# Hybrid retention and pooling block: the swish gate in seven-product units, retention and pooling input through DRAM, the retention merge ahead of the pooling branch

## The chip, the cores and the metric

The kernel runs on one core of a Trainium2 chip. The metric is device time in microseconds (us); the median of plain runs is compared, and one further execution is profiled. Times of one execution come from that profile.

## What is computed

One decoder block for one sequence of S = 1024 tokens, D = 1024 channels, all in float32. After an RMS norm with gain, one projection gives queries, keys and values of 4 retention heads, a swish gate g, 512 pooling channels pu and two gates of 1024:

```python
h = rmsnorm(x, ln_mix);  z = h @ w_in            # q | k | v | g | pu | gate_logits
ret   = retention_chunkwise(rotary(q) * 128**-0.5, rotary(k), v)      # chunks of 128
ret_n = groupnorm_per_head(ret) * gn_gain
y_ret = (silu(g) * ret_n) @ w_ret_up
y_pool = multiscale_pool(pu, pool_w, pool_scale) @ w_pool_up          # causal windows 2, 4, 8, 16
x = x + (sigmoid(g_A) * y_ret + sigmoid(g_B) * y_pool) @ w_o
x = x + relu(rmsnorm(x, ln_mlp) @ w_up)**2 @ w_down
out = rmsnorm(x, ln_f)
```

## The kernel before

Activations are kept feature-major: 128 features on the partitions, 1024 tokens in two halves of 512 (`sl`, `half`). A float32 operand is carried as a pair, a rounded high half (`split_pair`, L134, a copy on ScalarE) and a low half (L135, a subtraction on VectorE), and a product takes three passes: high by high, high by low, low by high (`PASSES`, `product`, L121). So a 128x512 result over 1024 inputs takes 8 x 3 = 24 matmuls (`feature_major`), that is 48 for both halves of a feature tile. The norm's 1/rms is not applied to h; it is in `R1`, by which results are multiplied afterwards.

`seven` (L177) is the other way to make products, one Strassen-like unit: a 1024x256 weight block is read as 2x2 blocks `a11, a12, a22, a21`, their sums s1 to s4 are made on VectorE (L188, into a tile of their own, `sum_...`), and seven products of 4 x 3 = 12 matmuls accumulate into the banks X, Y, Z and V: 84 matmuls make two feature tiles, which would take 96. The operands on the other side are the quarters of h and four sums of them, `hx`, which `mixed_blocks(k)` makes for k = 0 to 3: it loads two feature tiles of x again (`xw`, 1 MB, on POOL's DMA queue, L514, into a buffer of the weights' pool), scales them on ScalarE (L517), and makes four sums and their halves (L525, L135). A unit's results are read from the banks in `done`. With `late=True`, for the first unit, the first four products run over k = 0 to 2 first, and over k = 3 afterwards.

The stages, with their place in the profiled execution:

- 0 to 274 us: queries and keys (`rotary`), values (`ps_v`), and the retention of four heads (`retain`). Its end takes the group norm: statistics on VectorE, a power instruction on POOL (L441), the scaling on VectorE (L444), 64 transposes on TensorE (`ps_rt`, L454), and the result stays in SBUF as `retn`, 8 features.
- 225 to 371 us: `swish(f)` for 8 features (`ps_g`, 384 matmuls), between them `pool(g)` for 4 windows (`ps_pu`, 192 matmuls, then the window sums on VectorE), `pool_mix` (`ps_pw`, 24 matmuls) and `mixed_blocks`. The gated retention goes to `ret_dram`, the pooled result to `yp_dram`.
- 366 to 533 us: 8 gate units (`gates`, `ps_Xsg`, `ps_Ysg`, `ps_Zsg`, `ps_Vsg`; 672 matmuls). Their sigmoids go to `sg_dram`.
- 535 to 578 us: pooling merge (`ps_yp`, 192 matmuls), multiplied by its gate from `sg_dram` into `m` (L625). `ypf`, the pooled result, is loaded within the last gate unit.
- 578 to 665 us: retention merge (`ps_yr`, 384 matmuls), with `ret` loaded from `ret_dram` (L630), multiplied by its gate and added (L650, L651) into `mixT`.
- 665 to 753 us: output projection (`ps_o`, 384 matmuls) and the second norm: sums over the squares by matmul (`sums_b`), 1/rms on VectorE and POOL (`rstd_b`, L146, L147), spread by transposes (`spread_b`, L153).
- 754 to 1056 us: 16 seven-product units `up`, whose squared ReLU goes to `act_dram`; 1056 to 1380 us: the down projection by the same scheme (`ps_dnX` and so on, L854) and the last norm (`spread_z`).

Instructions are written stage by stage; the tile framework orders them on each engine by its own simulated timeline and sets the waits on buffers. The buffers are pools: `wpool` 4 buffers of 1 MB (weights, `xw`, `ret`), `rpool` 2 (raw weights), `apool` with tags `h` 16, `r` 16 and `a` 9 buffers of half a megabyte, PSUM 5 banks `mm` and 3 `aux`. DMA loads are queued on SP, stores and the `xw` loads on POOL.

## Time and profile before

| what | value |
|---|---|
| median of 3 plain runs | 1387.05 us (1386.79 to 1387.15) |
| profiled execution | 1388.35 us |
| its span | 1386.2 us |
| TensorE busy | 1365.0 us, 6584 instructions |
| VectorE busy | 967.1 us, 1590 instructions |
| ScalarE busy | 542.8 us, 903 instructions |
| mean granted TensorE clock | 0.995 of full speed |

A busy time is the sum of the stretches in which an engine runs an instruction. PE stands for TensorE, PEld for its weight loads, DVE for VectorE, ACT for ScalarE, POOL for GpSimd, SP for the queue that issues loads. "<-" in a wait points to what ended it; names in the trace have their numbers left out, so `w_sg` is any weight half of a gate unit.

### The profile page before, as it was taken

The numbers are of one execution on the slowest core, as the hardware profiler recorded it, in microseconds if no ns is written. First come the engines' busy times: TensorE is split into PE (matmuls) and PEld (weight loads), VectorE is DVE, ScalarE is ACT, GpSimd is POOL, SyncE is SP. The second block draws the span as 40 slices with busy tenths as digits, with TensorE's granted clock in tenths as the row PEclk, the third lists the DMA queues.
The fourth block names the chain that finished last, engine by engine and source line by source line (L and its number), as shares of the span: only waits on it lengthen the run. The fifth ranks groups of instructions, "written<-read, shape, count | busy, mean of one in ns | idle before, by whom it ended". The sixth has DMA issues, their size and how long they took to land.

```text
span 1386.2 us, 17348 instructions
## 1 busy us (share of the span) xinstructions
PE 1365.0 (98%) x6584; PEld 1146.2 (83%) x6584; DVE 967.1 (70%) x1590; ACT 542.8 (39%) x903; POOL 77.9 (6%) x136
## 2 busy tenths in 40 slices
PE   9999999999999999999999999999999999999997
PEld 6998999888788887888887888888887788888886
DVE  5766666778766746645467888777776977589574
ACT  6232324343333333322344343343332544444371
POOL 0000000100000000000000111101110000000000
PEclk9999999999999999999999999999999999999998
DMA  9111111223323328534322344334449986779431
GB/s 357 50 60 49 33 42 47 99 91 122 137 81 118 122 99 312 181 122 137 137 76 83 112 166 164 141 140 168 167 168 355 408 312 234 251 266 319 146 122 61
DMA packets 63490, 216.66 MB, mean 156 GB/s; under 512 B 7152, under 2 KB 9200, under 8 KB 59824
## 3 DMA queue, kind: packets, MB, share of 16 engines
q1 hardware_dynamic: 47568, 158.66, 32.7%
q0 software_dynamic: 15696, 56.89, 10.8%
q8 instruction: 51, 0.84, 0.2%
q14 instruction: 31, 0.25, 0.1%
q10 hardware_dynamic: 144, 0.03, 0.0%
HBM read 163.12 MB, written 52.43 MB: 155 GB/s over the span
## 4 chain that ended last, share of the span: by engine, by line
PE 91%; issue 5%; DVE 2%; DMA 1%; ACT 1%; POOL 0%; POOLq 0%; DVEq 0%; SPq 0%; ACTq 0%
PE ps_v L121 7%; PE ps_o L121 6%; PE ps_yr L121 6%; PE ps_Xup L195 6%; PE ps_Zup L195 6%; PE ps_dnX L854 6%; PE ps_dnZ L854 6%; PE ps_Vup L195 6%; PE ps_dnV L854 6%; PE ps_qT L121 3%; PE ps_g L121 3%; PE ps_yp L121 3%; PE ps_kT L121 3%; PE ps_Yup L195 3%; PE ps_Xsg L195 3%
## 5 line engine op out<-in xcount | busy, mean ns | idle before, releaser
L121 PE MATMUL ps_v<-w_v_hi,hT 128*128 128x256 f32 x512 | 95.9, 284 | 0.0
L854 PE MATMUL ps_dnX<-db,da 128*128 128x512 f32 x384 | 93.3, 390 | 2.6 <-ACT db L134 1.6
L195 PE MATMUL ps_Xup<-mv,w_up 128*128 128x512 f32 x384 | 93.8, 390 | 1.3 <-DVE w_up L135 1.3
L195 PE MATMUL ps_Vup<-mv,w_up 128*128 128x512 f32 x384 | 92.8, 389 | 0.0
L195 PE MATMUL ps_Zup<-mv,w_up 128*128 128x512 f32 x384 | 92.7, 389 | 0.0
L121 PE MATMUL ps_g<-hT,w_g 128*128 128x512 f32 x384 | 91.1, 392 | 0.0
L121 PE MATMUL ps_o<-mixT,w_o 128*128 128x512 f32 x384 | 87.5, 389 | 0.0
L854 PEld LDWEIGHTS ps_dnX<-db,da 128*128 128x128 f32 x384 | 71.8, 188 | 18.7 <-ACT db L134 2.0
L121 PE MATMUL ps_yr<-retT,w_ret 128*128 128x512 f32 x384 | 87.2, 389 | 0.0
L195 PEld LDWEIGHTS ps_Xup<-mv,w_up 128*128 128x128 f32 x384 | 71.9, 188 | 16.6 <-DVE w_up L135 1.8
L195 PEld LDWEIGHTS ps_Zup<-mv,w_up 128*128 128x128 f32 x384 | 72.1, 188 | 15.0
L121 PEld LDWEIGHTS ps_yr<-retT,w_ret 128*128 128x128 f32 x384 | 72.1, 188 | 15.0
L195 PEld LDWEIGHTS ps_Vup<-mv,w_up 128*128 128x128 f32 x384 | 72.1, 188 | 14.9
L121 PEld LDWEIGHTS ps_o<-mixT,w_o 128*128 128x128 f32 x384 | 72.0, 188 | 15.0
L121 PEld LDWEIGHTS ps_g<-hT,w_g 128*128 128x128 f32 x384 | 71.9, 189 | 14.7
L121 PEld LDWEIGHTS ps_v<-w_v_hi,hT 128*128 128x128 f32 x512 | 80.8, 192 | 0.0
L121 PE MATMUL ps_v<-w_v_lo,hT 128*128 128x256 f32 x256 | 72.7, 284 | 0.0
L730 ACT ACTIVATE act<-act 128x512 f32<-128x512 f32 x64 | 40.4, 632 | 71.7 <-DVE act L729 71.5
L134 ACT ACTIVATE w_up<-sum_up 128x512 fp32r<-128x512 f32 x64 | 40.2, 631 | 66.3 <-PE ps_Zup L195 27.3
L121 PE MATMUL ps_qT<-hT,w_qT 128*128 128x512 f32 x192 | 48.5, 398 | 1.4 <-ACT hT L138 1.1
L134 ACT ACTIVATE w_up<-raw_up 128x512 fp32r<-128x512 f32 x48 | 30.1, 630 | 49.1 <-PE ps_Zup L195 24.9
L121 PEld LDWEIGHTS ps_v<-w_v_lo,hT 128*128 128x128 f32 x256 | 49.1, 192 | 0.0
(251 smaller groups left out, 2811.6 us busy)
## 6 DMA issues: line engine op xcount, KB each, us to landing
...
raw_up<-in_w_up_dram SPq DMA_DIRECT2D x16, 1024.0 KB, 5.0
raw_sg<-in_w_gate_dram SPq DMA_DIRECT2D x8, 1024.0 KB, 4.9
...
```

Of the source, the lines that this page charges most:

```text
L121: nc.tensor.matmul(ps, stationary(k, sa), moving(k, sb), start=i == 0, stop=i == n - 1)
L134: nc.scalar.activation(dst[:, 0, :], src, AF.Copy)
L195: nc.tensor.matmul(ps, ws[x][:, sa, k * P : (k + 1) * P], moving[x][k][:, sb, :], start=start and k == 0 and n == 0, stop=k == 3 and n == ...
L730: nc.scalar.activation(dst, dst, AF.Square)
L854: nc.tensor.matmul(banks[i][:, c0 : c0 + n], w[:, sa, i * P : (i + 1) * P], x[:, sb, c0 : c0 + n], start=start and j == 0 and m == 0, stop ...
```

## The change

1. `seven` has no tile for the sums: s3 goes into a temporary tile with p1, u2 and u4, and s1, s2, s4 overwrite the raw blocks a21, a11 and a12. T2's product makes s3, s1 and s2, in this order. The up units use the same function.
2. The swish gate's projection is made by four more units: `mixer_unit(i)`, i = 0 to 3 for the swish gate, 4 to 11 for the two gates, all from one weight array `w_mix`. In `done`, a swish unit multiplies by R1 and the sign (one operation), takes the sigmoid on ScalarE, multiplies the normalized retention by gain and sigmoid, and by z.
3. `retain` returns the normalized chunks, with the scaling on ScalarE (and a small `nb` on VectorE). `transposed` writes each `retn` feature to `retn_dram`, on POOL's queue; the swish units load them back into their output tiles on the same queue. For head 3 it stands behind the pooling input and the mixed blocks, which now fill the time of this head's retention.
4. `pool_input(g)` makes only the pooling channels u, to `u_dram`. The windows and `ps_pw` have moved into the retention merge's loop, `pool(f // 2)` behind each odd f, and give `ypT` directly.
5. The retention merge (`ps_yr`) runs ahead of the pooling merge (`ps_yp`). `load_ret` is called within unit 11; the second gate is loaded in pairs (`sgb`) in the pooling merge, which adds and makes `mixT`.

As built, TensorE has 48 matmuls fewer, VectorE 32 additions or products more, ScalarE 48 activations more, POOL's queue 15 DMAs more and SP's 3 fewer.

```diff
@@ seven
-        sums = w_tile(f"sum_{name}", F32).rearrange("p (b j) -> p b j", b=4)
-        s1, s2, s3, s4 = (sums[:, i, :] for i in range(4))
+        tmp = w_tile(f"tmp_{name}", F32).rearrange("p (b j) -> p b j", b=4)
+        p1, u2, u4, s3 = (tmp[:, i, :] for i in range(4))
+        s1, s2, s4 = a21, a11, a12
...
-            T2: (Y, (s2, (s1, a21, a22), (s2, s1, a11))),
+            T2: (Y, (s2, (s3, a11, a21), (s1, a21, a22), (s2, s1, a11))),
             T1: (Z, (s1,)),
-            T3: (V, (s3, (s3, a11, a21))),
+            T3: (V, (s3,)),
@@ retain
+            nb = stat.tile([P, 4], F32, tag="nb", name=f"nb{h}_{half}", bufs=2)
+            nc.vector.scalar_tensor_tensor(nb, mv[:, :, 0], -1.0, rs, ALU.mult, ALU.mult)
             for t in range(4):
-                nc.vector.tensor_scalar(
-                    rt[:, t, :], rt[:, t, :], mv[:, t, 0:1], rs[:, t : t + 1],
-                    ALU.subtract, ALU.mult,
+                nc.scalar.activation(
+                    rt[:, t, :], rt[:, t, :], AF.Identity,
+                    bias=nb[:, t : t + 1], scale=rs[:, t : t + 1],
                 )
             rn.append(rt)
+        return rn
+
+    def transposed(h, rn):
...
-            retn.append(dst)
+            nc.gpsimd.dma_start(retn_dram[2 * h + e], dst)
@@ pooling input and mixed blocks
+    def pool_input(g):
+        w = load_piece(a["w_fm"][8 + g], f"w_pu{g}")
+        u = a_tile("a", f"u{g}")
+        for half in range(2):
...
+            feature_major(ps, w, hT, half)
+            nc.vector.tensor_tensor(u[:, sl], ps, R1[:, sl], ALU.mult)
+        nc.gpsimd.dma_start(u_dram[g], u)
...
-    for f in range(KT):
-        swish(f)
-        if 1 <= f <= 4:
-            pool(f - 1)
-        if 2 <= f <= 5:
-            pool_mix(f - 2)
-        if 1 <= f <= 4:
-            mixed_blocks(f - 1)
...
+    pool_input(0)
+    for g in range(1, 4):
+        pool_input(g)
+        mixed_blocks(g - 1)
+    mixed_blocks(3)
+    transposed(NH - 1, rn)
@@ units
+    def mixer_unit(i, late=False, after=None):
+        swish = i < 4
+        f0 = i if swish else (i - 4) // 4 * KT + i % 4
         tiles = (f0, f0 + 4)
+        o = [a_tile("h", f"mx{i}_{f}") for f in tiles]
+        if swish:
+            for m, f in enumerate(tiles):
+                nc.gpsimd.dma_start(o[m], retn_dram[f])
...
+            if swish:
+                nc.vector.scalar_tensor_tensor(z, y, sign, R1[:, sl], ALU.mult, ALU.mult)
+                nc.scalar.activation(sig, z, AF.Sigmoid)
+                nc.vector.scalar_tensor_tensor(
+                    dst, dst, vec[:, V_GNG + f : V_GNG + f + 1], sig, ALU.mult, ALU.mult
+                )
+                nc.vector.tensor_tensor(dst, dst, z, ALU.mult)
...
+    for i in range(12):
+        mixer_unit(i, late=i == 0, after=load_ret if i == 11 else None)
@@ merges
+    for f in range(KT):
+        w = load_piece(a["w_ret"][f], f"w_ret{f}")
+        m = a_tile("a", f"m{f}")
+        nc.sync.dma_start(m, sg_dram[f])
+        for half in range(2):
...
+            feature_major(ps, w, retT, half)
+            nc.vector.tensor_tensor(m[:, sl], m[:, sl], ps, ALU.mult)
+        mixed.append(m)
+        if f % 2:
+            pool(f // 2)
...
+            sg = w_tile(f"sgb{f}", F32).rearrange("p (i t) -> p i t", i=2)
+            nc.sync.dma_start(sg, sg_dram[KT + f : KT + f + 2].rearrange("i p t -> p i t"))
```

Where the order moves, three places. First VectorE (DVE) ahead of the first unit. Before, these rows stand among the last swish halves (`ps_g`, `retn`), with the sums and halves of gate unit 0 (`sum_sg0`, `w4_sg0`) and the last mixed operand (`hx6_3`):

```order
L537 TENSOR_TENSOR ps_g6_0_3322<-ps_g6_0_3322,R1_128 128x512
L135 TENSOR_TENSOR hx6_3_3236<-xw3_3219,hx6_3_3236 128x512
L188 TENSOR_TENSOR sum_sg0_3454<-raw_sg0_3452 128x512
L539 SCALAR_TENSOR_TENSOR retn3_0_2466<-retn3_0_2466,vec_101,sig6_0_3347 128x512
L188 TENSOR_TENSOR sum_sg0_3454<-raw_sg0_3452 128x512
L188 TENSOR_TENSOR sum_sg0_3454<-sum_sg0_3454,raw_sg0_3452 128x512
L542 TENSOR_TENSOR retn3_0_2466<-retn3_0_2466,ps_g6_0_3322 128x512
L188 TENSOR_TENSOR sum_sg0_3454<-raw_sg0_3452,sum_sg0_3454 128x512
L135 TENSOR_TENSOR w4_sg0_3475<-sum_sg0_3454,w4_sg0_3475 128x512
```

After, the same place has the last u product (`ps_pu3_1`) and the mixed operands of k = 3 among the sums of unit 0 (`tmp_mx0`, `raw_mx0`):

```order
L189 TENSOR_TENSOR tmp_mx0_2842<-raw_mx0_2840 128x512
L135 TENSOR_TENSOR hx5_3_2795<-xw3_2786,hx5_3_2795 128x512
L508 TENSOR_TENSOR xw3_2786<-xw3_2786 128x512
L189 TENSOR_TENSOR raw_mx0_2840<-raw_mx0_2840 128x512
L492 TENSOR_TENSOR u3_2712<-ps_pu3_1_2739,R1_128 128x512
L135 TENSOR_TENSOR hx4_3_2799<-xw3_2786,hx4_3_2799 128x512
L135 TENSOR_TENSOR w0_mx0_2847<-raw_mx0_2840,w0_mx0_2847 128x512
L135 TENSOR_TENSOR hx6_3_2803<-xw3_2786,hx6_3_2803 128x512
L189 TENSOR_TENSOR raw_mx0_2840<-raw_mx0_2840 128x512
L135 TENSOR_TENSOR w4_mx0_2862<-raw_mx0_2840,w4_mx0_2862 128x512
```

The swish products that stood between the operands of the units are gone from there, and the xw chain of k = 3 now stands directly ahead of the first unit's low half `w0_mx0`.

Second SP's queue at the end of the units. Before, the pooled results (`ypf`) and the gates (`m`) follow the last unit's weights:

```order
L179 DMA raw_sg7_4404<-in_w_gate_dram 128x2048
L604 DMA ypf0_4464<-yp_dram_2497 128x1024
L604 DMA ypf1_4472<-yp_dram_2497 128x1024
L604 DMA ypf2_4480<-yp_dram_2497 128x1024
L604 DMA ypf3_4488<-yp_dram_2497 128x1024
L620 DMA m0_4575<-sg_dram_3449 128x1024
```

After, it is the gated retention (`ret`, 1 MB each) and the gates of the retention branch:

```order
L179 DMA raw_mx11_4368<-in_w_mix_dram 128x2048
L569 DMA ret0_4427<-ret_dram_2834 128x2048
L569 DMA ret1_4441<-ret_dram_2834 128x2048
L614 DMA m0_4566<-sg_dram_2835 128x1024
L614 DMA m1_4625<-sg_dram_2835 128x1024
L569 DMA ret2_4455<-ret_dram_2834 128x2048
L614 DMA m2_4711<-sg_dram_2835 128x1024
L614 DMA m3_4770<-sg_dram_2835 128x1024
L614 DMA m4_4859<-sg_dram_2835 128x1024
L614 DMA m5_4918<-sg_dram_2835 128x1024
L569 DMA ret3_4469<-ret_dram_2834 128x2048
L614 DMA m6_5010<-sg_dram_2835 128x1024
```

The last quarter of the retention (`ret3`) is asked for behind six gate tiles.

Third TensorE at the first up unit. Before, the sums of the second half's squares (`sums_b1`) stand among matmuls of up units 0 and 1, and their spread follows after V, X and other groups:

```order
L163 MATMUL sums_b1_6083<-ones_97,sums2_5419 128x1 x4
L195 MATMUL ps_Vup0_6109<-mv5_3_6051,w5_up0_6149 128x512
L195 MATMUL ps_Xup1_6250<-mv0_0_5554,w0_up1_6254 128x512
L195 MATMUL ps_Xup1_6250<-mv0_1_5717,w0_up1_6254 128x512 x3
L195 MATMUL ps_Xup1_6250<-mv0_2_5880,w0_up1_6254 128x512 x3
L195 MATMUL ps_Vup0_6109<-mv5_3_6051,w5_up0_6149 128x512 x2
L195 MATMUL ps_Xup1_6250<-mv0_3_6043,w0_up1_6254 128x512 x3
L195 MATMUL ps_Xup0_6106<-mv1_3_6061,w1_up0_6169 128x512
L153 MATMUL spread_b1_6091<-ident_92,rstd_b1_6088 128x128 x4
L195 MATMUL ps_Yup0_6107<-mv4_0_5569,w4_up0_6124 128x512 x3
```

After, X of up unit 0 comes first, and four matmuls of Z and V stand between the sums and their spread:

```order
L153 MATMUL spread_b0_6138<-ident_92,rstd_b0_6135 128x128 x4
L196 MATMUL ps_Xup0_6165<-mv0_0_5615,w0_up0_6169 128x512 x3
L196 MATMUL ps_Xup0_6165<-mv0_1_5778,w0_up0_6169 128x512 x3
L196 MATMUL ps_Xup0_6165<-mv0_2_5941,w0_up0_6169 128x512 x3
L196 MATMUL ps_Xup0_6165<-mv0_3_6104,w0_up0_6169 128x512 x3
L163 MATMUL sums_b1_6144<-ones_97,sums2_5480 128x1 x4
L196 MATMUL ps_Zup0_6167<-mv3_0_5619,w3_up0_6196 128x512 x2
L196 MATMUL ps_Vup0_6168<-mv5_0_5623,w5_up0_6208 128x512 x2
L153 MATMUL spread_b1_6152<-ident_92,rstd_b1_6149 128x128 x4
L196 MATMUL ps_Yup0_6166<-mv4_0_5630,w4_up0_6184 128x512 x3
```

Between the sums and their spread stood 14 wide matmuls; now there are 4.

## Rows read from the trace of the kernel before

**Rows 1.** The page, part 1: busy us, share of the span, instructions.

```profile
PE 1365.0 (98%) x6584; PEld 1146.2 (83%) x6584; DVE 967.1 (70%) x1590; ACT 542.8 (39%) x903; POOL 77.9 (6%) x136
```

**Rows 2.** The page, part 4: chain that ended last, by engine.

```profile
PE 91%; issue 5%; DVE 2%; DMA 1%; ACT 1%; POOL 0%; POOLq 0%; DVEq 0%; SPq 0%; ACTq 0%
```

**Rows 3.** Waits of PE: what waited for what, us in total, times, longest.

```profile
PE spread_z L153 <- POOL rstd_z L147: 3.0, 2, 1.9
PE ps_yp L121 <- ACT w_po L94: 1.7, 1, 1.7
PE ps_dnX L854 <- ACT db L134: 1.6, 1, 1.6
PE ps_Ysg L195 <- ACT w_sg L134: 1.4, 1, 1.4
...
PE ps_dnX L854 <- DVE db L135: 1.1, 2, 0.8
...
PE ps_Zsg L195 <- DVE w_sg L135: 0.5, 1, 0.5
PE ps_pw L356 <- DVE pooled L135: 0.4, 2, 0.2
```

**Rows 4.** Timeline of PE: start, us, instructions; a key projection, transposes, a value matmul.

```profile
66.40 11.07 PE L121 MATMUL ps_kT<-hT,w_kT 128*128 128x512 f32 x48
77.31 0.60 PE L368 MATMUL ps_kt<-ident,kT 128*128 128x128 f32 x4
77.67 0.36 PE L121 MATMUL ps_v<-w_v_hi,hT 128*128 128x256 f32 x1
```

**Rows 5.** Windows: stretch, length; busy PE, PEld, DVE, ACT, POOL; PEclk; DMA share; GB/s.

```profile
368.70:371.70 3.00, 3.00 (x9) 2.32 (x8) 2.97 (x6) 0.76 (x2) 0.00 (x0) 0.50 0.13 52
534.70:537.70 3.00, 2.97 (x13) 2.45 (x14) 1.83 (x2) 1.72 (x3) 0.64 (x2) 1.00 0.84 244
756.70:759.70 3.00, 2.92 (x13) 2.40 (x14) 3.00 (x7) 0.93 (x2) 0.00 (x0) 1.00 0.12 49
1075.30:1078.30 3.00, 2.62 (x10) 1.88 (x11) 3.00 (x6) 2.23 (x5) 1.60 (x3) 1.00 1.05 416
224.60:366.40 141.80, 139.99 (x672) 116.63 (x670) 106.00 (x183) 56.47 (x91) 10.60 (x16) 1.00 0.30 103
366.40:532.60 166.20, 165.31 (x719) 136.04 (x720) 109.89 (x171) 64.41 (x105) 9.05 (x17) 0.99 0.34 123
```

**Rows 6.** Timelines of PE and PEld: the first gate unit, then the first up unit.

```profile
367.55 3.87 PE L195 MATMUL ps_Ysg<-hx,w_sg 128*128 128x512 f32 x10 [0.41 <-DVE w_sg L135]
371.22 2.09 PE L121 MATMUL ps_g<-hT,w_g 128*128 128x512 f32 x7
...
756.78 2.58 PE L195 MATMUL ps_Xup<-mv,w_up 128*128 128x512 f32 x10 [1.35 <-DVE w_up L135]
...
769.67 0.41 PEld L153 LDWEIGHTS spread_b<-ident,rstd_b 128*128 128x128 f32 x4 [0.26 <-POOL rstd_b L147]
```

**Rows 7.** Timeline of DVE: sums and low halves of gate units.

```profile
366.81 1.89 DVE L135 TENSOR_TENSOR w_sg<-sum_sg,w_sg 128x512 fp32r<-128x512 f32 x3
...
419.72 1.29 DVE L188 TENSOR_TENSOR sum_sg<-raw_sg 128x512 f32<-128x512 f32 x2
```

**Rows 8.** DMA issues (KB each, median us to landing), and the landings of ret.

```profile
xw<-in_xT_dram POOLq DMA_DIRECT2D x4, 1024.0 KB, 5.6
...
ret<-ret_dram SPq DMA_DIRECT2D x4, 1024.0 KB, 5.0
...
DMA to landing us min/median/max: 4.8/5.0/9.9
```

**Rows 9.** Timeline of POOL: the power instruction of the second norm.

```profile
768.21 1.41 POOL L147 TENSOR_TENSOR rstd_b<-rstd_b,nhalf 128x4 f32<-128x4 f32 x1 [12.98 <-DVE rstd_b L146]
```

**Rows 10.** Groups by line: busy, mean ns of one, idle before and what ended it.

```profile
L444 DVE TENSOR_SCALAR rn<-rn,mv,rs 128x256 f32<-128x256 f32 x32 | 11.0, 409 | 0.2
...
L517 ACT ACTIVATE xw<-xw,vec 128x1024 f32<-128x1024 f32 x8 | 8.8, 1142 | 30.8 <-DMA xw<-in_xT_dram 30.8
```

More of the change, by code (lines that the diff above doesn't have):

```diff
@@ L199, in mult @@
                     )
-        tmp = rpool.tile([P, 2, HALF], F32, tag="raw", name=f"tmp_{name}")
-        p1, u2 = tmp[:, 0, :], tmp[:, 1, :]
-        u4 = rpool.tile([P, HALF], F32, tag="raw", name=f"u4_{name}")
         X, Y = mm_bank(f"ps_X{name}"), aux_bank(f"ps_Y{name}")
@@ L358, in exact @@
             )
-    retn = []
+    retn_dram = dram_tile("retn_dram", (KT, P, S))
     def retain(h, qT, kT, v):
@@ L580, in done @@
             dst, f = o[m][:, sl], tiles[m]
+            sign = -1.0 if m else 1.0
+            if swish:
+                t = rpool.tile([P, 2, HALF], F32, tag="raw", name=f"sw{f}_{half}")
+                z, sig = t[:, 0, :], t[:, 1, :]
+            else:
+                z = ps if add is None else dst
             y = ps
             if add is not None:
-                nc.vector.tensor_tensor(dst, add, ps, ALU.add)
-                y = dst
-            nc.vector.tensor_tensor(y, y, R1[:, sl], ALU.mult)
@@ L611, in block_kernel, with load_ret @@
-    for i in range(KT):
-        gates(i)
-    mixed = []
+                nc.gpsimd.dma_start(ret_dram[f // 2, :, f % 2, :] if swish else sg_dram[f], o[m])
+        seven(f"mx{i}", a["w_mix"][i], hx, done, late=late, after=after)
+    retT = []
+    def load_ret():
+        for p2 in range(KT // 2):
+            r2 = w_tile(f"ret{p2}", F32).rearrange("p (i t) -> p i t", i=2)
+            nc.sync.dma_start(r2, ret_dram[p2])
+            for i in range(2):
+                retT.append([])
+                for half in range(2):
+                    dst = pair_tile("h" if p2 < 2 else "r", f"retT{2 * p2 + i}_{half}")
+                    split_pair(dst, r2[:, i, half * HALF : (half + 1) * HALF])
+                    retT[-1].append(dst)
@@ new lines, in block_kernel, with pool @@
+    for i in range(12):
+        mixer_unit(i, late=i == 0, after=load_ret if i == 11 else None)
+    pw_raw, pw = a_tile("r", "pw_raw", shape=(P, HALF)), pair_tile("r", "pw")
+    nc.sync.dma_start(pw_raw, a["pool_w"])
+    split_pair(pw, pw_raw)
+    ypT = []
+    def pool(g):
+        win = WINDOWS[g]
+        u = a_tile("r", f"uf{g}")
+        nc.sync.dma_start(u, u_dram[g])
+        cur = u
+        step = 1
+        while step < win:
+            nx = a_tile("r", f"s{g}_{step}")
+            nc.vector.tensor_copy(nx[:, :step], cur[:, :step])
+            nc.vector.tensor_tensor(nx[:, step:], cur[:, step:], cur[:, : S - step], ALU.add)
+            cur = nx
+            step *= 2
+        nc.vector.tensor_tensor(cur[:, :16], cur[:, :16], corr[:, g, :], ALU.mult)
+        nc.vector.scalar_tensor_tensor(cur, cur, 1.0 / win, u, ALU.mult, ALU.subtract)
+        ypT.append([])
+        for half in range(2):
+            pooled = pair_tile("r", f"pooled{g}_{half}")
+            split_pair(pooled, cur[:, half * HALF : (half + 1) * HALF])
+            ps = aux_bank(f"ps_pw{g}_{half}")
+            exact(ps, lambda s: pw[:, s, g * P : (g + 1) * P], lambda s: pooled[:, s, :])
+            dst = pair_tile("h", f"ypT{g}_{half}")
+            split_scaled(dst, ps, vec[:, V_PSC + g : V_PSC + g + 1])
+            ypT[g].append(dst)
@@ new lines, in block_kernel @@
+    mixed = []
+    for f in range(KT):
+        w = load_piece(a["w_ret"][f], f"w_ret{f}")
+        m = a_tile("a", f"m{f}")
+        nc.sync.dma_start(m, sg_dram[f])
+        for half in range(2):
+            sl = slice(half * HALF, (half + 1) * HALF)
+            ps = mm_bank(f"ps_yr{f}_{half}")
+            feature_major(ps, w, retT, half)
[3 more added lines that the diff above has]
+            pool(f // 2)
+    mixT = []
```

134 lines of the change are left out of this document (23 added, 111 removed).

## The prediction

> **What bounds the kernel now.** I read the page first. TensorE is busy for 1365.0 of 1386.2 us, VectorE for 70% and ScalarE for 39% [rows 1], and 91% of the chain that ended last is TensorE [rows 2]. So a matmul taken away is worth its whole pitch wherever TensorE is kept fed, and work on the other engines is free until TensorE waits for it. The list of TensorE's waits [rows 3] shows how little is left outside: the waits named in this text are single stalls of 0.2 to 1.9 us. They sit at seams, where one stage's operands are made while the last stage's matmuls run out. The prediction is therefore a count of matmuls and a walk over the seams that the change rebuilds.
>
> **Prices.** One projection of 48 matmuls of 512 columns runs from 66.40 to the first transpose at 77.31 [rows 4]: 10.91/48 = 0.227 us each. On VectorE two 128x512 sums take 1.29 us and three low halves 1.89 [rows 7]: each further one adds 0.60.
>
> **A, the removed matmuls.** The swish gate's 384 matmuls (8 features, 2 halves, 24 each) become four units of 84, 336 in all. 48 x 0.227 = **-10.9 us**. The pooling (192 + 24) and the group norm's 64 transposes keep their counts. Beside the measured pitch stands a page: the Trainium skill, "TensorE: Matmul & The Clock Gate", section "Wait — 56ns, not 53.3ns?", gives 215.7 ns from start to start of warm 512-column matmuls; this row, 227, is longer, and 48 of those would give 10.4.
>
> **What A costs on the other engines.** A swish unit has 28 half-row VectorE operations (4 last sums, 7 low halves, 2 corrections, 3 sums, 4 scalings, 4 gain products, 4 products): 28 x 0.60 = 16.8 us under 84 x 0.227 = 19.1 us of TensorE. It fits, with 2.3 us to spare. The neighbours have more room: in the swish and pooling stretch VectorE is busy 106.0 of 141.8 us, in the gates' stretch 109.9 of 166.2 [rows 5], that is 13.7 busy and 7.0 idle for each of its eight units. So I cost the extra work at nothing; if its cover is gone, it is rival 2. In-place sums make s1, s2, s4 overwrite the raw weights: a new wait for the raw tile's readers, all some 0.6 us VectorE or ScalarE steps of the same unit, ahead of matmuls that are queued a group later. Nothing.
>
> **Through DRAM.** Each retn feature gets a store and a load, each u too, on POOL's queue (POOL is busy for 6% of the span [rows 1]). A 1 MB load lands in 5.0 to 5.6 us [rows 8]; these are half as large, and the loads are asked for about a unit, 19 us, before the gain product reads them. Nothing again; without that cover about 5 us, once. On POOL the stores wait for the last copy of their tile, and behind them stand the power instruction (1.41 us [rows 9]) and the xw loads; this is rival 1. The scaling of rn, 32 operations of 0.409 us [rows 10], goes from VectorE to ScalarE; neither is waited for there. Merging the retention branch first swaps two stages of equal counts; the pool windows fall into the 384 matmuls of the retention merge, and the last ps_pw has the whole of ps_yr7 (48 matmuls, 10.9 us) to hide the last window. Nothing.
>
> **Seam B, pooling to units.** Before: a wait of 1.4 us at the first gate weights and 0.4 in two at ps_pw [rows 3], and 0.41 at the next gate matmuls [rows 6]. After them the granted clock reads 0.50, the lower level, from 368.7 to 371.7 [rows 5], and the ten matmuls from 367.55 end at 371.22 [rows 6]: 3.67 us where 10 x 0.227 = 2.27, so 1.40 lost. Together 3.6. After: from the end of ps_pu2_1 on, VectorE has 20 half-row operations (12.0 us) up to the low half of w0_mx0, and six tiny ones on statistics between them (some 0.6). TensorE covers these 12.6 with ps_pu3's 48 matmuls (10.9), retention's 16 transposes (four take 0.36 [rows 4], so 1.4) and the first 2 matmuls of X (0.45): 12.8. That is even at best, and VectorE comes to it late. I take the stall of the nearest row, 1.40 (the same kind of seam, same xw chain), and one spell at the lower clock, 1.4: 2.8, so **-0.8**. Bounds: clean, -3.6; a stall as long as an xw landing, 5.6 [rows 8], plus 1.4, +3.4.
>
> **Seam C, units to the merge.** Before: 1.7 at ps_yp, 0.5 at ps_Zsg [rows 3], 2.2. After, the merge starts with retT, whose last load needs the weight buffer that unit 11's last VectorE step frees: 0.69 + 5.0 [rows 8] + 0.63 for the split is 6.3 us, and ahead of retT6 stand 33 matmuls, 7.5 us. Covered; 0.5 stays for the small wait. **-1.7** (clean -2.2; with the slowest landing of such a load, 9.9 [rows 8], 11.2 - 7.5 = 3.7, +1.5).
>
> **Seam D, output projection to up.** The units' order is new there too. Before: 1.35 at ps_Xup and 0.26 at the second spread, 1.6 [rows 6]. After, the Z and V fillers (4 matmuls, 0.9) stand behind X, so X reaches its low half 0.9 earlier; one sum fewer is ahead of that half on VectorE, 0.6: 1.35 + 0.9 - 0.6 = 1.65. The second spread now comes 4 matmuls behind its sums, where it had far more. From the low half on, VectorE does six more steps (3.6) until the variance, POOL's power takes 1.4 [rows 9], in all 5.0 to 5.3; TensorE has the rest of X (2.3), the sums (0.4) and the fillers (0.9): 3.6. Left 1.6, between the 1.1 and 1.9 that TensorE waits for spread_z, two such places [rows 3]. 3.3 in all, **+1.7** (+0.5 to +2.5).
>
> **Seam E, up to down.** Before: 0.8 and 0.3 (1.1 in two) and 1.6 at ps_dnX [rows 3]: 2.6. After, the first down matmuls stand behind another Z group of 12, 2.7 us, which covers the first and most of the second. 0.8 left, **-1.8** (0 to -2.6).
>
> **Sum.** -10.9 - 0.8 - 1.7 + 1.7 - 1.8 = -13.5. The profiled execution took 1388.35 us (span 1386.2); 1388.35 - 13.5 = 1374.85. It is 1.30 above the median of the plain runs, 1387.05, so **1373.5 us** on their scale.
>
> **Rivals.**
> 1. *One xw round is exposed at seam B.* The xw buffers are shared with weights and the load waits on POOL behind stores. For: it took 5.6 us to land [rows 8], and 30.8 us of ScalarE's idle time ended on it before [rows 10]. Against: three of four are asked far ahead. It decides if xw3's load is issued later than the end of ps_pu2_1. Price: 5.6 + 2 x 1.14 scalings [rows 10] + 8 steps of 0.6 = 12.7 in place of 1.4: -2.2 in all, 1385.
> 2. *Slower: VectorE becomes the bound in the four swish units.* If VectorE keeps waiting 7.0 us a unit for TensorE and ScalarE, as in the gates [rows 5], while its work rises to 17, a unit takes 24 instead of 19.1: 5 x 4 = +20, so -13.5 + 20 = +6.5: 1393.5. It decides from 5.4 us of idle on (16.8 + 5.4 = 22.2: 3.1 lost in each, 12.4 in four, most of the gain). For: sigmoid, gain and product hang one on another. Against: they are read only by a store, and VectorE's queue holds the next unit's sums between them.
> 3. *All seams clean.* B, C and E at nothing, D at its lowest: -10.9 - 3.6 - 2.2 + 0.5 - 2.6 = -18.8; a good part of it, -18, gives 1369.
> 4. *The clock falls at each rebuilt seam.* It fell after 1.4 and 0.41 us of idle at 366 [rows 3, 6], but reads 1.00 after 1.7 at 534.7, 1.4 at 756.7 and 1.6 at 1075.3 [rows 5]; three falls of 1.4 give -9.3, 1377.7. [...]
>
> **How the numbers follow.** Forecast 0.62, rival 1 0.10, rival 2 0.06, rival 3 0.15, rival 4 0.07. About 0.2% (2.8 us) is what a measurement of this kernel can tell from no change: forecast, 3 and 4 are faster, 0.84; rival 1 is the same, 0.10; rival 2 slower, 0.06. The range: all lower bounds give -18.8 (1368), all upper ones -10.9 + 3.4 + 1.5 + 2.5 + 0 = -3.5 (1383.5 on the plain scale); few of these fall together, so 1368 to 1381, which holds 3 and 4 and leaves out 1 and 2.
>
> **What the profile after should show.** 48 fewer matmuls; no group ps_g, but X, Y, Z, V of four more units; TensorE's busy time some 11 us less, and still over 97% of the span. In a swish unit VectorE busy for about 17 of 19 us, no TensorE wait over 1 us inside it. At seam B one stall of 1 to 2 us and one stretch at 0.50; at C none over 1; at D one at ps_Xup and one at spread_b of some 1.6 each; at E one under 1. I am wrong if TensorE waits in the middle of swish units for sums or low halves (rival 2), if xw3 lands behind the last ps_pu (rival 1), or if the granted clock shows 0.50 at C, D or E (rival 4).

## The result and the profile after

| kernel | median us | lowest to highest | ratio to the kernel before |
|---|---|---|---|
| before | 1387.10 | 1386.79 to 1389.20 (4 runs) | 1 |
| changed | 1377.41 | 1375.46 to 1379.41 (4 runs) | 0.9927, 95% interval 0.9909 to 0.9945 |

The change makes the kernel 9.7 us faster by the medians (forecast 13.5, to 1373.5, range 1368 to 1381). The profiled execution of the changed kernel took 1375.46 us, 12.9 less than the 1388.35 of the profiled one before; it is the lowest of the four runs, and why the others are slower is a question of its own, which the first experiment takes up. The page, part 1, of the changed kernel, to be set beside [rows 1]:

```profile
PE 1352.9 (98%) x6536; PEld 1137.4 (83%) x6536; DVE 986.0 (72%) x1622; ACT 563.2 (41%) x951; POOL 86.2 (6%) x151
```

TensorE has 48 matmuls fewer and is busy for 12.1 us less; VectorE works 18.9 us more and ScalarE 20.4. The list of TensorE's waits (what waited for what: us in total, times, longest), to be set beside [rows 3]:

```profile
PE spread_z L153 <- POOL rstd_z L147: 3.7, 2, 2.6
PE ps_dnX L840 <- ACT db L134: 2.6, 1, 2.6
PE ps_Xup L196 <- DVE w_up L135: 1.7, 1, 1.7
...
PE ps_Zup L196 <- ACT w_up L134: 0.7, 1, 0.7
PE ps_rt L457 <- ACT retn L460: 0.7, 1, 0.7
...
PE ps_yr L121 <- ACT w_ret L94: 0.5, 1, 0.5
...
PE ps_Xmx L196 <- ACT w_mx L134: 0.3, 1, 0.3
```

Nothing in it waits inside the swish units. The stall in front of the pooling merge (ps_yp, 1.7) has become 0.5 in front of the retention merge (ps_yr); at the start of the up stage the waits have grown (ps_Xup, ps_Zup), and at its end one of 2.6 (ps_dnX) stands where there were 1.6 and two shorter ones, 1.1 together. The 3.7 of the last norm (spread_z) is 3.0 again in the second trace of this kernel.

To add up what a wait really costs, I took every pair of consecutive matmuls in the timeline of TensorE, subtracted the usual pitch of their kind (0.227 us for 512 columns) and summed what is left at each seam. What is left holds the wait, the refilling behind it and the time lost while the granted clock is low. The kernel was run once more as it is (first experiment), so two traces of it stand in this ledger, in us lost:

| seam | before | changed, 1375.46 us | changed, 1378.31 us | forecast difference |
|---|---|---|---|---|
| B, pooling to units | 5.0 | 2.9 | 5.8 | -0.8 |
| C, units to merge | 2.7 | 0.8 | 0.8 | -1.7 |
| D, output projection to up | 1.7 | 3.4 | 3.4 | +1.7 |
| E, up to down | 3.4 | 4.4 | 4.1 | -1.8 |
| start and last norm | 7.0 | 6.8 | 6.9 | 0 |
| whole kernel | 18.2 | 16.2 | 19.0 | -2.6 |
| pitch of all matmuls | 1360.3 | 1349.4 | 1349.4 | -10.9 |

(The line for the whole kernel also holds small gaps elsewhere, and pairs that follow closer than the usual pitch, 5 us in each trace, mostly transposes.) The pitch falls by 10.9 us in both; this line is a count of matmuls times their usual pitch, so it says that the pitch has not changed, and what else the change did is in the lines above it. The losses were to fall too; they fell by 2.0 in one execution and rose by 0.8 in the other: -12.9 and -10.1, which are the differences of the profiled times (1388.35 to 1375.46 and to 1378.31).

### The profile page after: what moved, and what is told of

Its sections match the earlier page's. It is cut to its first block, busy times and chain, and to the rows that moved or that the text cites. A ratio compares the mean times of both kernels' runs of the same rounds, so it can differ in the third digit from the quotient of the medians.

```text
span 1373.6 us, 17398 instructions
## 1 busy us (share of the span) xinstructions
PE 1352.9 (98%) x6536; PEld 1137.4 (83%) x6536; DVE 986.0 (72%) x1622; ACT 563.2 (41%) x951; POOL 86.2 (6%) x151
## 5 line engine op out<-in xcount | busy, mean ns | idle before, releaser
L134 ACT ACTIVATE w_up<-raw_up 128x512 fp32r<-128x512 f32 x96 | 58.3, 627 | 85.2 <-DVE raw_up L189 46.3
L196 PEld LDWEIGHTS ps_Zup<-mv,w_up 128*128 128x128 f32 x384 | 72.0, 188 | 15.7 <-ACT w_up L134 0.8
L135 DVE TENSOR_TENSOR w_up<-raw_up,w_up 128x512 fp32r<-128x512 f32 x96 | 64.5, 689 | 26.4 <-ACT w_up L134 26.1
L134 ACT ACTIVATE w_mx<-raw_mx 128x512 fp32r<-128x512 f32 x72 | 43.5, 627 | 85.6 <-DVE raw_mx L189 42.7
L196 PE MATMUL ps_Xmx<-hT,w_mx 128*128 128x512 f32 x288 | 70.4, 390 | 0.3 <-ACT w_mx L134 0.3
L196 PE MATMUL ps_Vmx<-hx,w_mx 128*128 128x512 f32 x288 | 69.5, 389 | 0.0
L196 PEld LDWEIGHTS ps_Xmx<-hT,w_mx 128*128 128x128 f32 x288 | 53.9, 188 | 12.1 <-ACT w_mx L134 0.6
```

The source lines that it names most:

```text
L134: nc.scalar.activation(dst[:, 0, :], src, AF.Copy)
L135: nc.vector.tensor_tensor(dst[:, 1, :], src, dst[:, 0, :].bitcast(F32), ALU.subtract)
L196: nc.tensor.matmul(ps, ws[x][:, sa, k * P : (k + 1) * P], moving[x][k][:, sb, :], start=start and k == 0 and n == 0, stop=k == 3 and n == ...
```

## The experiments

Each is timed beside the kernel before on the same chip. Three sets and one last kernel were run, on three chips; the medians of the kernel before were 1387.60, 1387.74, 1387.80 and 1389.31 us. The changed kernel itself was run in the first set alone, with a median of 1378.51 us; where a kernel of a later set is compared with it, the comparison is across sets, whose medians of the kernel before agree within 0.2 us.

### The changed kernel again

No edit.

> The changed kernel as it is, for its spread: its four runs so far lie between 1375.46 and 1379.41 us, with mean granted clocks between 0.996 and 0.993, where those of the kernel before lie within 0.3 us but for one. Theory 1, the clock: the difference is the number of seams at which the granted clock falls to the lower level after a stall. A mean clock lower by 0.001 of 1374 us stands for 2.75 us at half speed, so 1.4 us lost; a run 4 us above the fastest should show about 0.003 less, and the trace of a slower run should show 0.50 at a seam where the first trace shows 1.00. Median 1376 to 1379. Theory 2, transfers: the loads that share the memory with stores land later in some runs; then the time varies by microseconds at the same mean clock, and the stalls differ in length, not the clock behind them.

Measured: 1378.51 us (1376.68 to 1379.69), ratio 0.9929 (0.9916 to 0.9941). The mean granted clock lies between 0.992 and 0.995, and 0.995 belongs to the fastest run. At seam B the clock tells the two traces apart. Timeline of TensorE (start, us, instructions) in the first trace:

```profile
282.72 0.33 PE L457 MATMUL ps_rt<-ident,rn 128*128 128x128 f32 x1 [0.16 <-ACT rn L444]
283.72 0.66 PE L457 MATMUL ps_rt<-ident,rn 128*128 128x128 f32 x4 [0.67 <-ACT retn L460]
284.72 3.28 PE L196 MATMUL ps_Xmx<-hT,w_mx 128*128 128x512 f32 x12 [0.34 <-ACT w_mx L134]
```

and the window from there on (columns as in [rows 5]; the granted clock is the third figure from the end):

```profile
284.00:290.00 6.00, 5.66 (x26) 4.24 (x25) 2.68 (x5) 4.83 (x10) 1.12 (x3) 1.00 1.02 419
```

The same place in the second trace:

```profile
282.60 1.31 PE L457 MATMUL ps_rt<-ident,rn 128*128 128x128 f32 x7 [0.68 <-ACT rn L444]
284.08 0.33 PE L457 MATMUL ps_rt<-ident,rn 128*128 128x128 f32 x1 [0.16 <-ACT rn L444]
285.08 0.66 PE L457 MATMUL ps_rt<-ident,rn 128*128 128x128 f32 x4 [0.67 <-ACT retn L460]
286.08 4.78 PE L196 MATMUL ps_Xmx<-hT,w_mx 128*128 128x512 f32 x12 [0.34 <-ACT w_mx L134]
```

and its window:

```profile
286.00:290.00 4.00, 3.92 (x10) 2.82 (x11) 3.25 (x6) 3.52 (x8) 1.06 (x2) 0.58 0.97 396
```

In the second one TensorE has one more long wait for ScalarE among the transposes (0.68), and then X's twelve matmuls take 4.78 us instead of 3.28: the granted clock is 0.58 over that window, so most of it at the lower level, where the first trace has 1.00. The last mixed-operand load, asked for at 268.2 and 268.1, landed at 274.4 in the first trace and at 275.8 in the second. So both theories hold a part: the execution with the later transfer has the longer stall, by 1.3 us, and the fall of the clock behind it costs as much again, 1.5. Over the 50 runs of the kernel before that stood beside the experiments, time goes with the mean clock (correlation -0.93): 1385.6 to 1386.3 us at 0.997 (3 runs), 1387.1 to 1388.3 at 0.996 and 0.995 (23), 1388.3 to 1390.1 at 0.994 (19), 1391.0 to 1391.7 at 0.993 (4), 1392.1 at 0.991 (1). Each 0.001 is 1.1 us.

### A undone: the swish gate by plain products

The older product comes back as a function `swish_plain(f)`, left out here: it loads the retention from `retn_dram`, makes the 48 matmuls of a feature as in the kernel before, and stores.

```diff
-    for i in range(12):
-        mixer_unit(i, late=i == 0, after=load_ret if i == 11 else None)
+    def swish_plain(f):
...
+    for f in range(KT):
+        swish_plain(f)
+    for i in range(4, 12):
+        mixer_unit(i, after=load_ret if i == 11 else None)
```

> The swish gate alone goes back to 384 plain matmuls (48 for a feature, the retention loaded back from DRAM as in the changed kernel); all else is as changed. Theory 1: the 48 matmuls are worth their pitch, 48 x 0.227 = 10.9 us, so 10 to 12.5 us slower than the changed kernel, 1387 to 1390, and no wait of TensorE within the four swish units of the changed kernel disappears. Theory 2: part of the gain had been paid back in the swish units on VectorE: then less than 9 us slower.

Measured: 1389.83 us, 11.3 more than the changed kernel beside it. The pitch of its matmuls sums to 1360.3 us, 10.9 more, as in the kernel before. Seam B loses 1.0 there (plain products stand ahead of the first unit), 1.9 to 4.8 less than in the changed kernel; seam C loses 4.6, 3.8 more, in two waits for weights on ScalarE (1.55 and 0.94) and a fall of the clock behind them. The two seams move against each other, so that the time differs by so nearly the pitch is in part luck. The 48 matmuls are worth their pitch; without them the rest of the change is no gain (ratio to the kernel before 1.0012, 1.0003 to 1.0021).

### VectorE's cover in the swish units

```diff
                 nc.vector.tensor_tensor(dst, dst, z, ALU.mult)
+                for _ in range(1):
+                    nc.vector.tensor_tensor(z, z, sig, ALU.mult)
```

Nothing reads the added product.

> The changed kernel with four more VectorE products of 128x512 in every swish unit (z by the sigmoid, read by nothing). VectorE is busy for 17.4 to 19.0 of 19.0 us in the swish units of the changed kernel, 71.4 of 76.0 over the four. Theory 1, VectorE is near its limit there: 16 x 0.60 = 9.6 us more work, 4.6 of it finds room, the rest shows: 4 to 6 us slower than the changed kernel, with TensorE waiting for sums or low halves inside the swish units. Theory 2: its queue runs ahead into the gate units, which have 5 us of idle VectorE each: under 1.5 us slower.

Measured: 1381.45 us, 2.9 more than the changed kernel (of the set before). Windows of one unit's length over the swish units (292 to 368) in the changed kernel:

```profile
292.00:311.00 19.00, 19.00 (x85) 15.71 (x84) 17.42 (x29) 7.93 (x14) 0.00 (x0) 1.00 0.22 67
311.00:330.00 19.00, 19.00 (x85) 15.76 (x84) 19.00 (x32) 7.84 (x14) 2.13 (x4) 1.00 0.42 160
330.00:349.00 19.00, 19.00 (x85) 15.73 (x85) 17.60 (x30) 7.19 (x13) 2.13 (x4) 1.00 0.52 166
349.00:368.00 19.00, 19.00 (x86) 15.73 (x85) 17.43 (x30) 6.60 (x12) 1.07 (x2) 1.00 0.34 111
```

and the four windows from the second one on with the added work:

```profile
313.00:332.00 19.00, 19.00 (x85) 15.75 (x84) 17.53 (x30) 6.34 (x11) 2.12 (x4) 1.00 0.45 160
332.00:351.00 19.00, 19.00 (x85) 15.73 (x85) 19.00 (x32) 7.11 (x12) 2.13 (x4) 1.00 0.46 163
351.00:370.00 19.00, 19.00 (x86) 15.73 (x85) 17.59 (x30) 6.37 (x11) 1.06 (x2) 1.00 0.32 114
370.00:389.00 19.00, 19.00 (x86) 15.73 (x85) 18.11 (x31) 8.39 (x14) 1.59 (x3) 1.00 0.35 125
```

VectorE is the third figure behind the length. TensorE is busy without a gap in all of them. Of the 9.6 us of added work 8.3 show up behind the swish units: 18.1 and 15.7 us busy in the first two gate units instead of 14.4 and 11.1. So the units have no wait, as the second theory had it; it missed the sum. Most of the 2.9 us is seam C, which loses 3.4 instead of 0.8: the scheduler now puts the first weights of the retention merge behind the halves of its operands on ScalarE (wait of 2.67 us at ps_yr, 0.5 in the changed kernel). The order differs there from the changed kernel's; whether VectorE's load has a part in it is not separated.

### In-place sums alone, on the kernel before

```diff
-        sums = w_tile(f"sum_{name}", F32).rearrange("p (b j) -> p b j", b=4)
-        s1, s2, s3, s4 = (sums[:, i, :] for i in range(4))
+        tmp = w_tile(f"tmp_{name}", F32).rearrange("p (b j) -> p b j", b=4)
+        p1, u2, u4, s3 = (tmp[:, i, :] for i in range(4))
+        s1, s2, s4 = a21, a11, a12
...
```

> The kernel before with nothing but the in-place sums of the seven-product units (gates and up units), the smallest part of the change done alone. Theory 1: this part costs what the two seams of the up stage lost more in the changed kernel, whatever stands ahead: 1.7 us at its start (3.4 instead of 1.7) and 0.6 to 1.0 at its end (4.1 to 4.4 instead of 3.4): 1.5 to 3 us slower than the kernel before, 1389 to 1391. Theory 2: the losses come with the changed kernel's other parts (the merge's order, the loads at the end of it): within 1 us of the kernel before.

Measured: 1390.95 us beside 1389.31, ratio 1.0010 (1.0001 to 1.0019). Its trace loses 3.4 at seam D, the same as the changed kernel, and 6.9 at seam E, where the wait is 3.99 us and the clock stays low for longer. So the extra loss at D, and one at E at least as large as in the changed kernel, come with the in-place sums, whatever stands ahead.

### The up units with a tile of their own for the sums

The twelve mixer units keep the in-place sums, the sixteen up units call the older function.

> The up units alone go back to the older unit with a tile of its own for the sums; the twelve mixer units keep the in-place sums. Theory 1: the losses at the two seams around the up stage (1.7 us more at its start, 1.0 more at its end in the first trace) come from the order that the in-place sums give the scheduler: then the start returns to 1.7 us lost (from 3.4) and the end to 3.4 (from 4.4), and the kernel is 2 to 4 us faster than the changed one, near 1374. Theory 2: the first products of the up stage are late for what stands ahead of them (the norm, the loads), whatever unit follows: the same time within 1 us.

Measured: 1377.00 us (1374.62 to 1378.70), 1.5 less than the changed kernel, whose runs reach from 1376.68 to 1379.69; such a difference is not clear of the spread. Seam D loses 1.7 again, seam E 5.0 in its trace (1.0 and 4.0 at two stalls, as before the change, and with a fall of the clock behind the second). So the start is as expected; the end is not.

### The residual's loads held back

```diff
             x1[i + 4 * h] = t[:, h, :]
+            nc.vector.tensor_copy(t[:, h, 0:1], u2[3][:, 0:1])
             nc.sync.dma_start(t[:, h, :], x1_dram[i + 4 * h])
```

The copied column comes from a result of the first down sweep, so the load, which overwrites it, has to wait for that.

> The residual's loads (x1b, three of 1 MB ahead of the first down operands on SP's queue) are held back until the first sweep of the down projection is over, by a one-column copy into each tile ahead of its load. Theory 1: at the seam from up to down the first matmul waits 2.6 us because its activation tile takes 12.0 us to land behind x1b and four stores (7.3 us in the kernel before); without the 3 MB ahead, the loads are asked earlier and land in 5 to 8 us: the stall falls under 1 us, the clock stays up behind it, 3 to 4 us faster than the changed kernel, near 1374. Theory 2: the first down loads wait for buffers that the last up unit frees and collide with its stores anyway: stall and time stay within 1 us.

Measured: 1374.97 us (1374.58 to 1375.44), 3.5 less than the changed kernel, and with a small spread. The seam in the changed kernel, in order of time: SP's queue with the loads of the first operands, POOL's with the stores of an up unit, TensorE and ScalarE (timeline: start, us, what):

```profile
1028.48 5.08 SPq L749 DMA_DIRECT2D x1b<-x_dram  x4
1033.66 0.38 SPq L753 DMA_DIRECT2D wa_lo<-in_w_down_dram  x1
1033.87 0.53 POOL L728 DMA_DIRECT2D act_dram<-act  x1 [13.50 <-issue]
1034.08 1.32 SPq L762 DMA_DIRECT2D wa_hi<-in_w_down_dram  x2
1034.39 0.53 POOL L727 DMA_DIRECT2D act_dram<-act  x1
...
1035.52 0.49 SPq L770 DMA_DIRECT2D ad<-act_dram  x1
...
1042.73 2.88 PE L196 MATMUL ps_Zup<-mv,w_up 128*128 128x512 f32 x12
1047.53 0.63 ACT L134 ACTIVATE db<-ad 128x512 fp32r<-128x512 f32 x1 [5.18 <-DMA ad<-act_dram]
1048.21 3.88 PE L840 MATMUL ps_dnX<-db,da 128*128 128x512 f32 x9 [2.60 <-ACT db L134]
```

ScalarE sits idle for 5.18 us until `ad`, asked for at 1035.52, lands at 1047.5: 12.0 us. The stall of TensorE is followed by the lower clock (window, granted clock third from the end):

```profile
1048.00:1052.00 4.00, 3.79 (x10) 3.03 (x11) 3.81 (x7) 2.37 (x6) 0.00 (x0) 0.57 1.03 411
```

In the kernel before, `ad` was asked for 1.2 us ahead of these stores, and landed after 7.3:

```profile
1038.81 6.01 SPq L763 DMA_DIRECT2D x1b<-x_dram  x4
1047.22 0.37 SPq L784 DMA_DIRECT2D ad<-act_dram  x1
1048.38 0.53 POOL L742 DMA_DIRECT2D act_dram<-act  x1 [16.09 <-ACT act L730]
```

With x1b held back:

```profile
1029.34 0.33 SPq L754 DMA_DIRECT2D wa_lo<-in_w_down_dram  x1
1036.82 0.80 SPq L763 DMA_DIRECT2D wa_hi<-in_w_down_dram  x2
1037.72 0.37 SPq L771 DMA_DIRECT2D ad<-act_dram  x1
...
1044.74 0.63 ACT L134 ACTIVATE db<-ad 128x512 fp32r<-128x512 f32 x1 [1.28 <-DMA ad<-act_dram]
1046.82 2.88 PE L196 MATMUL ps_Zup<-mv,w_up 128*128 128x512 f32 x12
1049.54 2.20 PE L841 MATMUL ps_dnX<-db,da 128*128 128x512 f32 x9
```

`ad` lands after 7.0 us and TensorE passes from ps_Zup to ps_dnX without a wait; the seam loses 0.4 (one stall of 0.28 at 1063.8). The rest of the table's E, some 1.7 us, was the clock: the nine matmuls behind the stall took 3.88 us, here 2.20.

The landing goes with the place of `ad` among the stores. Counted from the last Z group, the stores leave at the same moment as in the changed kernel and `ad` 1.9 us earlier, now 0.23 us ahead of the first store (1037.96). All fourteen traces divide so. In seven, two of the four stores leave 1.0 to 1.7 us ahead of `ad` and a third within 0.1 us of it, and it lands after 11.7 to 13.5 us. In the other seven it leaves ahead of all four and lands after 5.7 to 7.4; two of these, the kernel before and up_own_sums, have the x1b loads ahead of `ad` as closely as the changed kernel has (2.8 us, where it has 2.4) and land it in 7.3. So x1b ahead does not by itself make the landing long; without it `ad` leaves early enough. No trace has the stores ahead without x1b.

### Both edits together

x1_late on the kernel with the older up units.

> Both edits of the last set on the changed kernel: x1b held back behind the first down sweep, and the up units with a tile of their own for the sums. Theory 1: the two seams are independent; the start of the up stage loses 1.7 us as in the kernel before (x1_late alone: 3.4 and a fall of the clock, 4.95), and the end loses 0.4 to 1.5: 1.5 to 3 us faster than x1_late, 1372 to 1373.5. Theory 2: the older unit frees its buffers later, so the down loads are late again at the end of the up stage (4 to 5 us lost there, as in up_own_sums): no faster than x1_late, 1375 to 1377.

Measured: 1378.71 us (1374.22 to 1380.17), 3.7 more than x1_late. The second theory's loss comes about, its reason does not: seam D loses 1.7, seam E 5.1, of the same form as in up_own_sums. With sums of their own the last up units interleave with the first down rows in another order, as before the change, and run into a wait of 1.57 for ScalarE there. ScalarE itself stands idle for 3.17 us until VectorE has an up result, and the halves for the next down matmuls come behind that; their loads had landed by then, and the first `ad` took 5.7 us. x1b has no part in this stall.

### The last head's transposes behind the first unit

```diff
-    transposed(NH - 1, rn)
...
         mixer_unit(i, late=i == 0, after=load_ret if i == 11 else None)
+        if i == 0:
+            transposed(NH - 1, rn)
```

> The changed kernel with the last head's transposes and stores behind the first mixer unit in the program instead of ahead of it. In the changed kernel the seam into the units lost 2.4 us in one trace and 5.3 in the other; the last mixed-operand load landed at 274.4 in the one and 275.8 in the other. Theory 1: from that landing on ScalarE does everything in turn (two scalings, halves, eight scalings of rn, copies of the transposes) ahead of the first weights; without rn and the copies there the first weights come 3 us earlier and the seam loses under 2 us: 1 to 3 us faster than the changed kernel. Theory 2: the transposes are only cover for a wait on VectorE; without them TensorE waits as long, for the low half of the first weights: within 1 us.

Measured: 1376.64 us, 1.9 less than the changed kernel. Seam B loses 3.1 (2.4 and 5.3 without its small wait at 264): X starts 0.5 us behind ps_pu, but Y now waits 1.7 for its weights on ScalarE. The gain is at the edge of what such a difference can tell, no gain shows at this seam in a trace without a fall of the clock (2.4 in the changed kernel), and the loss is not the under 2 us of the first theory.

### The scaling of rn on VectorE

The older `tensor_scalar` (L444 of the kernel before) in place of the activation.

> The changed kernel with the group norm's scaling back on VectorE (the rest as changed). I costed that move at nothing. Theory 1: at the seam into the units ScalarE is the engine that TensorE waits for (rn and retn, 0.9 to 1.7 us in the two traces); eight operations less there, eight of 0.41 us more on VectorE, which has the first low half in the same queue: within 1.5 us either way, with the waits for rn gone and the wait for the low half longer. Theory 2: the move off VectorE is what keeps this seam short: 2 to 4 us slower.

Measured: 1378.80 us, 0.3 more than the changed kernel, as the first theory had it. Waits for rn are gone from seam B, X's low half is late by 1.2 instead, 5.4 lost in its trace, with a fall of the clock as in the trace that lost 5.3. The move off VectorE is worth nothing either way.

### The gains together, and the mixed operands earlier

late_first2_rt: x1b held back, the older function for the first two up units alone, transposes behind the first unit. late_first2_mb: the first two of these, and

```diff
     pool_input(0)
-    for g in range(1, 4):
-        pool_input(g)
-        mixed_blocks(g - 1)
-    mixed_blocks(3)
+    pool_input(1)
+    mixed_blocks(0)
+    mixed_blocks(1)
+    pool_input(2)
+    mixed_blocks(2)
+    mixed_blocks(3)
+    pool_input(3)
```

late_first2_mb_rt: this order, with the transposes behind the first unit.

> The edits that gave a gain, together: x1b held back (x1_late), the first two up units with a tile of their own for the sums and the other fourteen with in-place sums, the last head's transposes behind the first mixer unit (rt_after0). Theory 1: each of the three seams keeps what it lost in its own experiment: 3.1 into the units, 1.7 into the up stage (5.0 in x1_late, 3.4 in the changed kernel), 0.4 into the down stage (4.0 in x1_late_up_own, whose up units all had a tile of their own): 1372 to 1374. Theory 2: it is the first unit that decides the end of the stage too, by the order it sets off: 4 lost at the end, 1376 to 1378.

> x1b held back, the first two up units with a tile of their own, and the mixed blocks written ahead of the last pooling input (input 0, 1, blocks 0, 1, input 2, blocks 2, 3, input 3); the transposes stay ahead of the first unit. In the changed kernel xw3 is asked for at 268.1 and lands at 274.4 to 275.8, and the seam into the units loses 2.4 to 5.3. Theory 1: the seam hangs on that landing; if xw3 is asked for 8 to 10 us earlier, the seam loses under 1.5 us, 1371 to 1374. Theory 2: the mixed operands need buffers that retention frees at 264, and the last weights now wait for a buffer: TensorE waits ahead of ps_pu3 instead, nothing gained or some us lost, 1375 to 1380.

> As the kernel with the mixed blocks written earlier, with the last head's transposes behind the first mixer unit as well. Theory 1 (ScalarE's work ahead of the first weights counts as much as the landing of xw3): the seam loses under 1 us and the run is the fastest of all, 1370 to 1373. Theory 2 (the transposes are cover): as the kernel with the transposes ahead of the first unit, within 1 us.

Measured: 1371.83 us (1370.09 to 1373.59) for the first, ratio 0.9880 (0.9864 to 0.9896): it beats both kernels, by 16.0 and 6.7 us (the changed kernel is from the first set). Its trace loses 3.5 at B, 0.8 at C, 1.7 at D and 0.4 at E, 12.6 in all: the seams keep their own losses, as the first theory had it. What the moved transposes add to this is not separated. The seam into the up stage in the changed kernel (timeline of TensorE):

```profile
741.19 2.56 PE L196 MATMUL ps_Xup<-mv,w_up 128*128 128x512 f32 x10 [1.67 <-DVE w_up L135]
743.59 0.95 PE L163 MATMUL sums_b<-ones,sums 128*128 128x1 f32 x8
745.27 0.73 PE L196 MATMUL ps_Zup<-mv,w_up 128*128 128x512 f32 x2 [0.74 <-ACT w_up L134]
```

and in late_first2_rt:

```profile
740.75 0.72 PE L262 MATMUL ps_Xup<-mv,w_up 128*128 128x512 f32 x2
741.30 0.62 PE L262 MATMUL ps_Zup<-mv,w_up 128*128 128x512 f32 x2
741.76 0.63 PE L262 MATMUL ps_Vup<-mv,w_up 128*128 128x512 f32 x2
743.74 2.58 PE L262 MATMUL ps_Xup<-mv,w_up 128*128 128x512 f32 x10 [1.35 <-DVE w_up L135]
```

The fillers (two Z and two V matmuls, whose high halves are ready) are ahead of the wait again.

The other two took 1376.85 and 1375.87 us, the times of their second theories. TensorE waits ahead of the last pooling input, for its weights (late_first2_mb, timeline):

```profile
272.72 1.19 PE L121 MATMUL ps_pu<-hT,w_pu 128*128 128x512 f32 x4 [2.03 <-ACT w_pu L94]
276.14 12.38 PE L121 MATMUL ps_pu<-hT,w_pu 128*128 128x512 f32 x44 [2.23 <-DVE w_pu L95]
...
293.23 3.76 PE L196 MATMUL ps_Xmx<-hT,w_mx 128*128 128x512 f32 x10 [1.67 <-DVE w_mx L135]
```

The buffer of the theory is not what the trace shows. ScalarE stands idle until xw3 lands at 269.5, scales it, and makes the high half of these weights behind that, from 271.6; VectorE comes to the low half at 274.9, behind statistics and mixed operands. The two waits and a fall of the clock cost 6.9 us.

These two kernels tell something of seam B all the same. The last load was asked for 4.7 us earlier (263.4) and landed at 269.5, long before it was needed, and X still waited 1.67 us for VectorE; with the transposes moved as well nothing is lost at the seam. So B does not hang on that landing alone, but on the queue of halves, sums, scalings and copies on VectorE and ScalarE together. In the order of the changed kernel, though, the landing goes with the loss from one execution to the next. Six traces have that order at B; xw3 took 6.2, 6.6, 6.9, 7.5, 7.5 and 7.7 us to land in them, and the seam lost, without its small wait at 264 and the time at the lower clock, 2.4, 2.8, 3.3, 3.6, 3.5 and 3.7 us. A fall of the clock added 1.4 to 1.7 us in three of the six.

## Why the prediction was right, and where not

The direction and the range were right, and 72% of the size: -9.7 of -13.5 by the medians, -12.9 in the profiled pair. That the profiled pair comes so near is in part luck: there seam B came out 1.3 us better than forecast, which hides half of the 2.8 by which seam E came out worse. By its steps:

- **A** (-10.9) holds: the usual pitch is 0.227 in both kernels, the four units run without a gap, and undoing them costs 11.3 us.
- **VectorE's cover** (16.8 of 19.1 us a unit) was a little short: 17.4 to 19.0 are busy. It holds because the queue runs ahead into the next units, which the added work showed. Rival 2 is out, and its price was wrong in kind: idle time that a unit has is filled by the next one's work.
- **Through DRAM, and merging ahead**: no wait of TensorE for either. C gave -1.9 (forecast -1.7).
- **D** (+1.7) is exact in its sum and in its first term: fillers behind X cost 1.67 at ps_Xup (forecast 1.65). The rest is 0.74 at ps_Zup rather than a wait of 1.6 at the second spread, so one term stood in the wrong place, and that the sum agrees is in part luck. in_place_alone shows that this loss belongs to the in-place sums.
- **E** (-1.8) is the step that failed: +1.0 and +0.7 in the two traces, with a stall of 2.6 and 2.3 us where "at E one under 1" was to show. "the first down matmuls stand behind another Z group of 12, 2.7 us, which covers the first and most of the second" counted only what stands ahead on TensorE. The Z group is there (ps_Zup, 12 matmuls at 1042.73), but the operand was late: in the new order the load of `ad` leaves behind the first stores of a unit instead of ahead of them, and 7.3 us to landing became 12.0. TensorE waits as long as before there, 2.6 us in one stall instead of in three, where 0.8 was forecast, and the clock falls behind that one stall, which costs 1.7 more; in the ledger the seam is 2.5 to 2.8 us off the forecast. x1_late puts `ad` ahead of the stores again, and the seam loses 0.4, less than the 0.8 of the forecast: the cover was counted rightly, the landing was not counted at all. By the medians x1_late gains 3.5 us, of the 3.8 that the forecast was off.
- **B** (-0.8, from a stall of 1.4 and one spell at the lower clock) came out at -2.1 in the trace without a fall of the clock and +0.8 in the one with it; the forecast lies between, but the wait was another. It had TensorE waiting for VectorE's low half. Both traces have it waiting for ScalarE instead, for rn, for the copies `retn` and for the first high half, and of the scaling of rn on ScalarE the prediction says "neither is waited for there". rn_dve takes that wait away and gets the one for the low half (1.2), for the same time. Rival 1 did not come about: xw3 was asked for at 268.1 to 268.3, and ps_pu2_1 ended at 269.9 (48 matmuls, 10.9 us, before 280.8). Its landing does go with the length of the stall.
- **Rival 4**, the clock, has some truth. By the prediction's own sign, 0.50 at C, D or E, it was wrong at E: the clock fell there in both traces. It fell at B in one, at C and D in neither; in x1_late it fell at D, behind the same stall as in the changed kernel, where it had not fallen (x1_late, window):

```profile
744.00:753.00 9.00, 8.19 (x34) 6.34 (x33) 8.84 (x17) 4.75 (x10) 1.41 (x1) 0.81 0.06 25
```

The Trainium skill, "TensorE: Matmul & The Clock Gate", section "HAM oscillation — how this bites in real kernels", describes a kernel in which TensorE waits for a transfer in every tile and starts each next tile at the lower clock. Its waits are longer than those of the changed kernel, and here no such regularity shows: a mean of 0.57 behind 2.6 us at E, but 1.00 behind 1.67 and 0.74 at D, and 0.81 behind the same two waits in x1_late. So the clock is a possible extra loss at each seam and no fixed term of the sum.

## What to carry to other kernels

Where TensorE is busy for 98% of the span, a removed matmul is worth its pitch, and the rest of a change is decided at the seams between stages. At a seam, ask for every operand of the next stage when its load is issued, behind which other transfers, and how long the nearest such load took under that company; a stage that moves can put its loads beside stores that they used to precede. Check with the order what stands ahead of a wait as filler, since a smaller buffer scheme can take it away.

## What the runs showed of the chip

The spread between executions of one kernel, 6.5 us of 1387 from the lowest to the highest of 50 runs, goes with the mean granted clock: 1.1 us for each 0.001. Traces put it at the seams and at the start: after a stall of 1 to 3 us the clock falls from its upper level (2.4 GHz) to its lower one (1.2 GHz) in some executions and not in others, and each fall costs 1.4 to 1.8 us. A wait of 2.67 us at seam C of swish_dve4 had no fall behind it, one of 2.6 at seam E of the changed kernel had. The start loses 2.0 to 2.1 us in the six traces in which the clock rises once there, and 3.2 to 3.6 in the eight in which it falls back once more, at 7.5 to 9.1 us. So removing a stall of 2.3 to 2.6 us at E gave 3.5; the four runs of that kernel lie within 0.9 us, though its own trace has two other falls, at the start and at D.

Transfers of one kind took 5.7 to 13.5 us to land at the same place of the kernel, by whether stores had been issued just ahead of them. `ad`, half a megabyte, took 7.0 in x1_late and 7.3 before, ahead of all stores of the unit, and 12.0 in the changed kernel and 13.5 in in_place_alone, behind the first two of the unit's four stores (three of half a megabyte, one of a quarter) and together with the third. Between 1038 and 1050 us of the changed kernel 356 to 420 GB/s were moved.
